# Experts' stage of a one-layer backbone kernel: the low half of U is made ahead of the gathered steps, the stage's first loads are asked for in another order, and its pools wait for their own bytes

## The chip, the cores and the metric

One NeuronCore of one Trainium2 chip runs the whole kernel. The metric is device time in microseconds (us) of one execution, the median of a few. The engines are TensorE (PE; its weight loads are shown as PEld), VectorE (DVE), ScalarE (ACT), GpSimd (POOL) and SyncE (SP). Each runs its own instructions in program order and waits on semaphores for the others. DMA transfers are asked for by SyncE and, for the gathers, by GpSimd; 16 DMA engines carry them.

## What is computed

One layer over 1024 tokens of width 1024: a mixer (state-space heads and a convolution group), and behind it a retrieval network over 16384 experts, each of which is one row of `u_tab` and one of `v_tab`. The change concerns the last part alone:

```python
q = (hf @ wq).reshape(t, PEER_HEADS, 2, PEER_KEY_DIM // 2)
s = einsum("thpd,hpkd->thpk", q, sub_keys)
sv, si = top_k(s, 16)                        # per half key, then over the 256 pairs
best, flat = top_k(cand, 16)                 # 8 heads x 16 experts for each token
gates = softmax(best)
act = gelu(einsum("pd,ped->pe", xb, u_tab[eb]), approximate=False)
out = einsum("pe,ped->pd", gb * act, v_tab[eb])
```

then `x + mod * out` and a final RMS norm.

## The kernel before, in words

The tokens lie in eight tiles of 128. In front of the experts' stage the **selection** finds each token's 128 experts and gates (`select`, L1016), for seven tiles; its pools `tp2`, `spl`, `gst` and two PSUM pools are closed before the stage opens its own. `prepare` (L994) already splits the activations (`hh2`, `hl2`) and multiplies expert block 0; it asks for U of blocks 0 to 3.

The **experts' stage** (L1241 on) has two kinds of work for two sets of tokens.

*Dense, for the first five tiles (640 tokens).* All 16384 experts are multiplied, in 128 blocks of 128, with gates that are zero where an expert was not chosen. A block's `In` step (L1358) has these parts: `load` brings U of the block (512 KB, SyncE), `split` makes its high half `uh` (ScalarE), `lower` its low half `ul` = u - uh (VectorE, L982), `gate` brings the gates of two blocks `gm` (640 KB, SyncE), `mm` multiplies (TensorE, 48 matmuls of 320 columns in groups of 8; the first 8 need `uh`, the next 8 `ul`), `post` is the gelu (ScalarE, L1392), `weigh` multiplies by the gates (VectorE, L1396) and makes the high half `wh` (ScalarE), `low` the low half `wl` (VectorE, L1402). An `Out` step (L1404) brings 256 KB of V, splits it into `vh` (ScalarE) and `vl` (VectorE, L61) and multiplies 15 times with 512 columns. `seq` (L1475) sets their order: 8 `In`, then for each of 16 groups 8 `Out`, one `In`, 8 `Out`, seven `In`.

*Gathered, for the last three tiles.* `gathered` (L1272) is a generator. For each token tile it asks GpSimd to gather 128 rows of `u_tab` (one expert of each token, 512 KB a request, L1281), lets VectorE multiply each with the activations h2 (L1303), and then does the same with rows of `v_tab` (L1315): 768 gathers, 5 buffers `gr`. The selection of the eighth tile (`choosing`, L1340) also runs here, in small pieces on VectorE and GpSimd; it reads its scores `s` from DRAM.

The order of every engine's queue is the order in which Python emits the instructions. `mm` of an `In` calls `advance(2, 18)`, that of an `Out` `advance(1, 11)` (L1347): as many pieces of the selection, and gathered steps in proportion to 18 and 11 (788 steps in 5066 units: 2.8 and 1.7 steps). Thus the gathered steps stand on VectorE's queue between `weigh` and `low` of the block before. The main loop (L1504) is:

```python
before.weigh()            # the In in front, if there is one
passed[type(x)] += 1
begin(In, "gate", 2)
x.mm()                    # TensorE, and advance() on VectorE and GpSimd
before.low()
begin(In, "lower", 1)     # ul of the next In
begin(In, "load", NU + 1)
x.post()
```

`begin(kind, what, far)` does that part for the steps up to `far` ahead. Blocks 0 to 3 are multiplied or prepared ahead of the loop, so the first `In` that multiplies in the loop is block 3, and block 4 is the first whose U is loaded in it.

A tile is given its place by its pool: the buffers lie in the order in which the names are first asked for. The stage's pools lie where the selection's lay, from the same byte on: `ep2` over `tp2` and part of `spl`, the gathers' `gp` over `gst`. In `tp2` the order is `iotx`, `v`, `ix`, `scr` (4 KB so far), `o1` (4 KB), `cand` (3.1 KB), `best`, `pos`, `posf`, `ef`, and so on. `gm` has two buffers of 5 KB for each partition, `v` three of 2 KB. By default the first use of a pool's memory waits until all users of the pools under it are through.

Of the kernel before, what the change touches and what calls it, by code (L numbers as in the profile page):

```python
# [8 lines left out]
F32 = mybir.dt.float32  # L9
# [6 lines left out]
PSUM = bass.MemoryType.PSUM  # L16
DRAM = bass.MemoryType.DRAM

P = 128
# [20 lines left out]
TH = TD // 2  # L40
NS = 7
NGB = 5
IN_US, OUT_US = 18, 11
NU, NV = 3, 3
GE = 8
# [27 lines left out]
def layer_kernel(ctx, tc, A, dbg=None):  # L73
# [293 lines left out]
    with ExitStack() as st:  # L367
# [126 lines left out]
        for n, c in enumerate(order):  # L494
# [13 lines left out]
            elif c >= 16 and c < 20:  # L508
                i = c - 16
# [458 lines left out]
    U = {}  # L968
# [6 lines left out]
    def split_u(u):  # L975
        uh = e2.tile([P, KD, P], F32R, name="uh")
        ul = e2.tile([P, KD, P], F32R, name="ul")
        nc.scalar.activation(uh, u, AF.Copy)  # L978
        return uh, ul, u

    def lower_u(uh, ul, u):
        nc.vector.tensor_tensor(ul, u, uh.bitcast(F32), op=OP.subtract)  # L982
        return uh, ul
# [255 lines left out]


    with ExitStack() as st:  # L1241
        ep2 = st.enter_context(tc.tile_pool(name="ep2", bufs=2))
        tp1 = st.enter_context(tc.tile_pool(name="tp1", bufs=1))
        wpl = st.enter_context(tc.tile_pool(name="wpl", bufs=GE + 1))
        gp = st.enter_context(tc.tile_pool(name="gp", bufs=NGB))
        psV = st.enter_context(tc.tile_pool(name="psV", bufs=1, space=PSUM))
        acc = h2T[:, :ND]
        h2, ac, spare = (h2T[:, ND + i] for i in range(3))
        spare_w, spare = spare, spare.rearrange("p (k t) -> p k t", t=P)
# [22 lines left out]
        def gathered():  # L1272
# [4 lines left out]
            def ask():  # L1277
                if asks:
                    t, b, e = asks.pop(0)
                    g = gp.tile([P, D], F32, name="gr")  # L1280
                    nc.gpsimd.indirect_dma_start(out=g, out_offset=None, in_=A[t],  # L1281
                                                 in_offset=bass.IndirectOffsetOnAxis(ap=idx[:, b, e:e + 1], axis=0))
                    rows.append(g)

            nc.sync.dma_start(h2, h2n_dram[:P, :])
            for _ in range(NGB - 2):
                ask()
            for b in range(NT - ND):
                act = ep2.tile([P, P], F32, name="act")
                wv = ep2.tile([P, P], F32, name="wv")  # L1290
# [29 lines left out]
            yield from done  # L1320

        steps = gathered()
        units = [0, 0]

        SE = {}

        def bring(z, hh):
            SE[z, hh] = tp1.tile([P, 4, P], F32, name="s", bufs=2)
            nc.sync.dma_start(SE[z, hh].rearrange("p a b -> p (a b)"), sc_dram[z - NS, hh])
# [8 lines left out]
            return tp1.tile([P, 2, TOPK], F32, name="ef"), heads(gates[:, z - ND], h0, 2)  # L1338

        def choosing():  # L1340
            bring(NS, 0)
            for z in range(NS, NT):
                yield from select(z, tp1, 2, scored, put)

        choice = choosing()

        def advance(n, us):  # L1347
# [128 lines left out]
        for g in range(NG):  # L1476
# [3 lines left out]
            seq += [Out(g, 1, i) for i in range(GE)]  # L1480
            if g + 1 < NG:
                seq += [In((g + 1) * GE + i) for i in range(1, GE)]
        early = [psV.tile([P, 512], F32, name=f"pv{i}")[:, :TH] for i in range(4)]
        for e in (1, 2):
            if e > 1:
                U[e] = lower_u(*split_u(U[e]))
            done[e] = multiply_u(*U.pop(e), early[2 * e - 2:2 * e])
        U[3] = lower_u(*split_u(U[3]))
        passed = {In: 0, Out: 0}
        queues = {(kind, what): iter([x for x in seq if isinstance(x, kind)]) for kind, what in  # L1490
                  ((In, "load"), (In, "split"), (In, "lower"), (In, "gate"), (Out, "load"), (Out, "split"))}
# [2 lines left out]
        def begin(kind, what, far):  # L1494

            while begun[kind, what] < passed[kind] + far:
                begun[kind, what] += 1
                x = next(queues[kind, what], None)
                if x:
                    getattr(x, what)()  # L1500

        begin(In, "load", NU + 1)
        begin(Out, "load", NV)
        for n, x in enumerate(seq):  # L1504
            begin(In, "split", 2)
            begin(Out, "split", 2)
            begin(Out, "load", NV + 2)
            before = seq[n - 1] if n and isinstance(seq[n - 1], In) else None
            if before:
                before.weigh()  # L1510
            passed[type(x)] += 1
            begin(In, "gate", 2)
            x.mm()
            if before:
                before.low()
            begin(In, "lower", 1)
            begin(In, "load", NU + 1)
            x.post()
        for _ in steps:
            pass  # L1520
# [75 lines left out]
```

## Time and profile before

| | before |
|---|---|
| median of 3 runs | 3130.14 us (3124.53 to 3130.31) |
| profiled execution | 3129.54 us, span 3127.7 us |
| TensorE busy | 2841.5 us, 91% |
| VectorE busy | 2632.5 us, 84% |
| GpSimd, ScalarE busy | 1713.4 us, 1011.7 us |
| DMA | 722.65 MB, 231 GB/s over the span |

By stretches of the experts' stage:

| us from the span's start | TensorE busy | VectorE busy | granted clock | DMA share |
|---|---|---|---|---|
| 1203 to 1260 | 38.37 of 57 | 33.33 | 0.78 | 0.72 |
| 1260 to 1700 | 404.26 of 440 | 376.30 | 0.96 | 0.84 |
| 1700 to 3040 | 1322.57 of 1340 | 1155.31 | 1.00 | 0.94 |
| 3040 to 3128 | 60.26 of 88 | 57.38 | 0.83 | 0.37 |

All times are from one profiled execution and count from its start. A busy TensorE is not TensorE at its peak: matmuls overlap, and their ends are modelled. "Waited for" names the instruction whose semaphore came last. The granted clock is the share of TensorE's full rate: 1.0 is 2.4 GHz, 0.5 is 1.2 GHz.

### The profile page before, as it was taken

How to read it: one execution, taken by the hardware profiler on the slowest of the kernel's cores; microseconds unless marked ns; L12 is line 12 of the kernel's file. 1: busy time of each engine (PE TensorE's matmuls, PEld its weight loads, DVE VectorE, ACT ScalarE, POOL GpSimd, SP SyncE). 2: the span in 40 equal slices, each digit the busy share in tenths (PEclk: the TensorE clock that was granted, in tenths of full speed). 3: DMA queues.
4: the chain of work that ended last, by engine and by line, in shares of the span. 5: the costliest groups of instructions: out<-in, count | busy, mean ns of one | idle time of the engine just before them, and what ended most of it. 6: DMA issues, size and time to landing. Idle time of an engine off the chain costs nothing.

```text
span 3127.7 us, 41600 instructions
## 1 busy us (share of the span) xinstructions
PE 2841.5 (91%) x14905; PEld 2381.7 (76%) x14905; DVE 2632.5 (84%) x4956; ACT 1011.7 (32%) x1584; POOL 1713.4 (55%) x1361
## 2 busy tenths in 40 slices
PE   7999777998888875999989999999999999999996
PEld 3777676764555555887878988998998898898885
DVE  5898788559999997889888888888888888888886
ACT  3224323333555652232222222222222322222222
POOL 0221454425676774666666666565566555556663
PEclk8999999999999887999999999999999999999998
DMA  6111355250222125888879999999998998999983
GB/s 209 61 40 42 112 150 184 81 188 7 115 108 108 55 122 199 286 277 314 297 273 326 320 336 339 328 334 326 327 334 315 328 349 314 334 335 322 327 290 127
DMA packets 334543, 722.65 MB, mean 231 GB/s; under 512 B 24560, under 2 KB 167168, under 8 KB 333056
## 3 DMA queue, kind: packets, MB, share of 16 engines
q0 software_dynamic: 112176, 408.47, 36.8%
q1 hardware_dynamic: 222160, 311.53, 29.0%
q8 instruction: 117, 1.92, 0.2%
q14 instruction: 90, 0.74, 0.1%
HBM read 658.56 MB, written 61.35 MB: 230 GB/s over the span
## 4 chain that ended last, share of the span: by engine, by line
PE 44%; DVE 29%; issue 10%; DMA 8%; POOL 6%; ACT 2%; SPq 0%; DVEq 0%; POOLq 0%; ACTq 0%
PE pa L990 18%; PE pv L1428 5%; PE pv L1429 5%; PE pv L1427 5%; POOL gr L1281 4%; DMA gr<-in_peer_u_dram,idx 4%; DVE cfm L408 3%; DVE o L1211 3%; PE pa L68 3%; DVE ob L1203 2%; PE pq L947 2%; DVE oh L1081 2%; DMA gr<-in_peer_v_dram,idx 2%; DVE gr L1303 1%; DVE h2T L1315 1%
## 5 line engine op out<-in xcount | busy, mean ns | idle before, releaser
L1281 POOL DMA_INDIRECT gr<-in_peer_v_dram,idx x384 | 537.6, 1400 | 325.5 <-DVE h2T L1315 219.1
L1281 POOL DMA_INDIRECT gr<-in_peer_u_dram,idx x384 | 523.8, 1364 | 347.9 <-DVE gr L1303 262.5
L1428 PE MATMUL pv<-vl,wh 128*128 128x512 f32 x1280 | 513.4, 401 | 26.0 <-DVE vl L61 25.9
L1315 DVE SCALAR_TENSOR_TENSOR h2T<-gr,wv,h2T 128x1024 f32<-128x1024 f32 x381 | 495.7, 1301 | 38.3 <-DMA gr<-in_peer_v_dram,idx 31.5
L1427 PE MATMUL pv<-vh,wl 128*128 128x512 f32 x1280 | 510.6, 399 | 7.2 <-ACT vh L60 7.0
L1303 DVE SCALAR_TENSOR_TENSOR gr<-gr,h2T 128x1024 f32<-128x1024 f32 x384 | 463.9, 1235 | 57.5 <-DMA gr<-in_peer_u_dram,idx 52.8
L1429 PE MATMUL pv<-vh,wh 128*128 128x512 f32 x1280 | 510.7, 399 | 0.0
L60 ACT ACTIVATE vh<-v 128x512 fp32r<-128x512 f32 x256 | 161.8, 632 | 682.6 <-PE pv L1429 656.1
L990 PE MATMUL pa<-hh,ul 128*128 128x320 f32 x2000 | 340.3, 313 | 40.1 <-DVE ul L982 39.2
L990 PE MATMUL pa<-hl,uh 128*128 128x320 f32 x2000 | 336.8, 311 | 8.3 <-ACT uh L978 8.3
L990 PEld LDWEIGHTS pa<-hh,ul 128*128 128x128 f32 x2000 | 306.6, 190 | 45.4 <-DVE ul L982 44.4
L990 PE MATMUL pa<-hh,uh 128*128 128x320 f32 x2000 | 337.6, 311 | 0.0
L990 PEld LDWEIGHTS pa<-hl,uh 128*128 128x128 f32 x2000 | 307.8, 190 | 11.3 <-ACT uh L978 8.6
L1428 PEld LDWEIGHTS pv<-vl,wh 128*128 128x128 f32 x1280 | 243.2, 190 | 92.4 <-DVE vl L61 35.7
L990 PEld LDWEIGHTS pa<-hh,uh 128*128 128x128 f32 x2000 | 307.5, 190 | 0.0
L1392 ACT ACTIVATE ga<-pa 128x320 f32<-128x320 f32 x252 | 110.0, 438 | 594.7 <-PE pa L990 571.0
L1427 PEld LDWEIGHTS pv<-vh,wl 128*128 128x128 f32 x1280 | 243.6, 190 | 66.4 <-ACT vh L60 8.2
L1429 PEld LDWEIGHTS pv<-vh,wh 128*128 128x128 f32 x1280 | 243.4, 190 | 57.8
L1205 POOL TENSOR_TENSOR o<-ob,tr 128x512 f32<-128x512 bf16 x160 | 216.5, 1355 | 110.7 <-DVE ob L1203 99.4
L1189 PEld LDWEIGHTS pg<-o,o 128*128 128x128 f32 x1280 | 173.9, 207 | 132.5 <-issue 66.4
L61 DVE TENSOR_TENSOR vl<-v,vh 128x512 fp32r<-128x512 f32 x256 | 184.4, 721 | 105.1 <-ACT vh L60 104.1
L1189 PE MATMUL pg<-o,o 128*128 128x128 f32 x1280 | 187.4, 297 | 78.8 <-DVE o L1211 53.9
(357 smaller groups left out, 4510.3 us busy)
## 6 DMA issues: line engine op xcount, KB each, us to landing
v<-in_peer_v_dram SPq DMA_DIRECT2D x256, 256.0 KB
u<-in_peer_ut_dram SPq DMA_DIRECT2D x87, 512.0 KB
g_dram<-stg SPq DMA_DIRECT2D x10, 4096.0 KB
gm<-g_dram SPq DMA_DIRECT2D x64, 640.0 KB
h2T<-in_peer_ut_dram SPq DMA_DIRECT2D x41, 512.0 KB
ld<-in_ada_w_dram SPq DMA_DIRECT2D x24, 512.0 KB
w<-in_w_in_t_dram SPq DMA_DIRECT2D x21, 512.0 KB
raw<-in_ada_w_dram SPq DMA_DIRECT2D x8, 1024.0 KB
```

Of the source, the lines that this page charges most:

```text
L60: nc.scalar.activation(hi, src, AF.Copy)
L61: (eng or nc.vector).tensor_tensor(lo, src, hi.bitcast(F32), op=OP.subtract)
L990: nc.tensor.matmul(pa[half], x[:, k], y[:, k, half * TH:half * TH + TH], start=t == 0 and k == 0, stop=t == 2 and k == KD - 1)
L1189: nc.tensor.matmul(pg[:, j], o2[:, j], o1[:, j], start=True, stop=True)
L1205: nc.gpsimd.tensor_tensor(o2.rearrange("p t j -> p j t"), ob, tr[:, 1, None, ts].to_broadcast([P, P, 4]), op=OP.mult)
L1281: nc.gpsimd.indirect_dma_start(out=g, out_offset=None, in_=A[t], in_offset=bass.IndirectOffsetOnAxis(ap=idx[:, b, e:e + 1], axis=0))
L1303: nc.vector.scalar_tensor_tensor(g, g, 1.0, h2, op0=OP.mult, op1=OP.mult, accum_out=act[:, e:e + 1])
L1315: nc.vector.scalar_tensor_tensor(ac, g, wv[:, e:e + 1], ac, op0=OP.mult, op1=OP.add)
L1392: nc.scalar.activation(self.ga[:, half * TH:half * TH + TH], self.pa[half], AF.Gelu)
L1427: nc.tensor.matmul(Out.pv[t], wl[:, sl], self.vh, start=i == 0, stop=False)
L1428: nc.tensor.matmul(Out.pv[t], wh[:, sl], self.vl, start=False, stop=False)
L1429: nc.tensor.matmul(Out.pv[t], wh[:, sl], self.vh, start=False, stop=i == GE - 1)
```

## The change

Four things move; nothing is added to or taken from the arithmetic.

- The five pools of the stage are opened with `reuse_waits="tile"`: the first use of a buffer waits for the users of the bytes under it, not for all users of the pools that lay there.
- `gathered` now stops once behind its first requests (h2 on SyncE, three gathers on GpSimd), and it is run to that point where it is made; the first scores of the eighth tile (`bring(NS, 0)`) are asked for there too.
- The first gates (blocks 0 to 2, two `gm` tiles) are asked for ahead of the first V tiles, and all these loads ahead of the multiplications of blocks 1 and 2 in the program.
- In the loop, `lower` and the load of U stand between `weigh` of the block before and `mm`.

```diff
@@ -1239,11 +1239,11 @@
 
 
     with ExitStack() as st:
-        ep2 = st.enter_context(tc.tile_pool(name="ep2", bufs=2))
-        tp1 = st.enter_context(tc.tile_pool(name="tp1", bufs=1))
-        wpl = st.enter_context(tc.tile_pool(name="wpl", bufs=GE + 1))
-        gp = st.enter_context(tc.tile_pool(name="gp", bufs=NGB))
-        psV = st.enter_context(tc.tile_pool(name="psV", bufs=1, space=PSUM))
+        ep2 = st.enter_context(tc.tile_pool(name="ep2", bufs=2, reuse_waits="tile"))
+        tp1 = st.enter_context(tc.tile_pool(name="tp1", bufs=1, reuse_waits="tile"))
+        wpl = st.enter_context(tc.tile_pool(name="wpl", bufs=GE + 1, reuse_waits="tile"))
+        gp = st.enter_context(tc.tile_pool(name="gp", bufs=NGB, reuse_waits="tile"))
+        psV = st.enter_context(tc.tile_pool(name="psV", bufs=1, space=PSUM, reuse_waits="tile"))
         acc = h2T[:, :ND]
         h2, ac, spare = (h2T[:, ND + i] for i in range(3))
         spare_w, spare = spare, spare.rearrange("p (k t) -> p k t", t=P)
@@ -1285,6 +1285,7 @@
             nc.sync.dma_start(h2, h2n_dram[:P, :])
             for _ in range(NGB - 2):
                 ask()
+            yield
             for b in range(NT - ND):
                 act = ep2.tile([P, P], F32, name="act")
                 wv = ep2.tile([P, P], F32, name="wv")
@@ -1320,6 +1321,7 @@
             yield from done
 
         steps = gathered()
+        next(steps)
         units = [0, 0]
 
         SE = {}
@@ -1338,10 +1340,10 @@
             return tp1.tile([P, 2, TOPK], F32, name="ef"), heads(gates[:, z - ND], h0, 2)
 
         def choosing():
-            bring(NS, 0)
             for z in range(NS, NT):
                 yield from select(z, tp1, 2, scored, put)
 
+        bring(NS, 0)
         choice = choosing()
 
         def advance(n, us):
@@ -1480,27 +1482,28 @@
             seq += [Out(g, 1, i) for i in range(GE)]
             if g + 1 < NG:
                 seq += [In((g + 1) * GE + i) for i in range(1, GE)]
+        passed = {In: 0, Out: 0}
+        queues = {(kind, what): iter([x for x in seq if isinstance(x, kind)]) for kind, what in
+                  ((In, "load"), (In, "split"), (In, "lower"), (In, "gate"), (Out, "load"), (Out, "split"))}
+        begun = dict.fromkeys(queues, 0)
+
+        def begin(kind, what, far):
+
+            while begun[kind, what] < passed[kind] + far:
+                begun[kind, what] += 1
+                x = next(queues[kind, what], None)
+                if x:
+                    getattr(x, what)()
+
+        begin(In, "gate", 3)
+        begin(In, "load", NU + 1)
+        begin(Out, "load", NV)
         early = [psV.tile([P, 512], F32, name=f"pv{i}")[:, :TH] for i in range(4)]
         for e in (1, 2):
             if e > 1:
                 U[e] = lower_u(*split_u(U[e]))
             done[e] = multiply_u(*U.pop(e), early[2 * e - 2:2 * e])
         U[3] = lower_u(*split_u(U[3]))
-        passed = {In: 0, Out: 0}
-        queues = {(kind, what): iter([x for x in seq if isinstance(x, kind)]) for kind, what in
-                  ((In, "load"), (In, "split"), (In, "lower"), (In, "gate"), (Out, "load"), (Out, "split"))}
-        begun = dict.fromkeys(queues, 0)
-
-        def begin(kind, what, far):
-
-            while begun[kind, what] < passed[kind] + far:
-                begun[kind, what] += 1
-                x = next(queues[kind, what], None)
-                if x:
-                    getattr(x, what)()
-
-        begin(In, "load", NU + 1)
-        begin(Out, "load", NV)
         for n, x in enumerate(seq):
             begin(In, "split", 2)
             begin(Out, "split", 2)
@@ -1510,11 +1513,11 @@
                 before.weigh()
             passed[type(x)] += 1
             begin(In, "gate", 2)
+            begin(In, "lower", 1)
+            begin(In, "load", NU + 1)
             x.mm()
             if before:
                 before.low()
-            begin(In, "lower", 1)
-            begin(In, "load", NU + 1)
             x.post()
         for _ in steps:
             pass
```

## Rows read from the trace of the kernel before

**Rows 1.** The page, part 1: busy us (share of the span) and instructions.
```profile
PE 2841.5 (91%) x14905; PEld 2381.7 (76%) x14905; DVE 2632.5 (84%) x4956; ACT 1011.7 (32%) x1584; POOL 1713.4 (55%) x1361
```

**Rows 2.** TensorE's waits, 1205 to 1262: waiter, for whom: us, times, longest.
```profile
PE pa L990 <- DVE ul L982: 10.1, 1, 10.1
PE pa L990 <- ACT uh L978: 8.3, 1, 8.3
```

**Rows 3.** The same view, 1262 to 1700.
```profile
PE pa L990 <- DVE ul L982: 20.4, 5, 7.3
PE pv L1428 <- DVE vl L61: 13.4, 5, 5.5
```

**Rows 4.** The same view, 1700 to 3040.
```profile
PE pa L990 <- DVE ul L982: 8.8, 11, 1.7
```

**Rows 5.** SyncE in order of time: start us, us, instruction. Start of the stage.
```profile
1202.83 0.33 SPq L972 DMA_DIRECT2D u<-in_peer_ut_dram  x1
1211.33 9.19 SPq L1413 DMA_DIRECT2D v<-in_peer_v_dram  x5
1220.58 1.69 SPq L1371 DMA_DIRECT2D gm<-g_dram  x2
...
1233.52 0.62 SPq L1285 DMA_DIRECT2D h2T<-h2n_dram  x1
```

**Rows 6.** VectorE in order of time, same stretch; in brackets its wait before.
```profile
1210.94 0.22 DVE L1099 CAST idx<-ef 128x128 int32<-128x128 f32 x1
...
1228.25 0.82 DVE L1396 TENSOR_TENSOR ga<-ga,gm 128x640 f32<-128x640 f32 x1 [8.09 <-DMA gm<-g_dram]
...
1245.14 1.22 DVE L982 TENSOR_TENSOR ul<-u,uh 128x1024 fp32r<-128x1024 f32 x1
```

**Rows 7.** TensorE in order of time, same stretch.
```profile
1233.86 2.50 PE L990 MATMUL pa<-hl,uh 128*128 128x320 f32 x8 [8.35 <-ACT uh L978]
1246.41 2.50 PE L990 MATMUL pa<-hh,ul 128*128 128x320 f32 x8 [10.05 <-DVE ul L982]
```

**Rows 8.** GpSimd in order of time, same stretch.
```profile
1207.80 1.61 POOL L1083 TENSOR_TENSOR oh<-oh,cand 128x160 f32<-128x160 f32 x2 [0.32 <-DVE oh L1081]
```

**Rows 9.** Stretches: length, engines' busy us, granted clock, DMA share, GB/s.
```profile
1194.00:1203.00 9.00, 4.24 (x15) 3.56 (x14) 8.90 (x28) 0.00 (x0) 6.01 (x6) 0.51 0.02 5
...
1228.00:1234.00 6.00, 0.14 (x1) 0.14 (x1) 3.94 (x5) 3.89 (x8) 0.00 (x0) 0.52 0.56 200
```

**Rows 10.** DMA queues, 1216 to 1222: packets, MB, share (q0 GpSimd's, q1 SyncE's).
```profile
q0 software_dynamic: 437, 1.61, 70.5%
q1 hardware_dynamic: 347, 0.64, 29.6%
```

**Rows 11.** ScalarE in order of time, start of the stage.
```profile
1218.81 0.63 ACT L60 ACTIVATE vh<-v 128x512 fp32r<-128x512 f32 x1 [2.85 <-DMA v<-in_peer_v_dram]
...
1220.75 0.77 ACT L1392 ACTIVATE ga<-pa 128x320 f32<-128x320 f32 x2
...
1232.75 1.06 ACT L978 ACTIVATE uh<-u 128x1024 fp32r<-128x1024 f32 x1
```

**Rows 12.** TensorE's waits, 1480 to 1520.
```profile
PE pa L990 <- DVE ul L982: 7.6, 3, 4.7
```

**Rows 13.** VectorE in order of time, around 1505.
```profile
1501.06 0.81 DVE L1396 TENSOR_TENSOR ga<-ga,gm 128x640 f32<-128x640 f32 x1
...
1510.03 1.23 DVE L1303 SCALAR_TENSOR_TENSOR gr<-gr,h2T 128x1024 f32<-128x1024 f32 x1 [1.77 <-DMA gr<-in_peer_u_dram,idx]
...
1511.91 1.22 DVE L982 TENSOR_TENSOR ul<-u,uh 128x1024 fp32r<-128x1024 f32 x1
```

**Rows 14.** The chain that ended last: start us, us, instructions. TensorE, two pieces.
```profile
1349.58 7.05 PE pa L990 x48
...
1391.47 7.94 PE pa L990 x40
```

**Rows 15.** VectorE's waits, 1700 to 3040.
```profile
DVE ga L1396 <- ACT ga L1392: 48.8, 60, 2.1
```

More of the change, by code (lines that the diff above doesn't have):

```diff
@@ L1482, in layer_kernel @@
                 seq += [In((g + 1) * GE + i) for i in range(1, GE)]
[L1483 to L1488, printed above, removed]
         passed = {In: 0, Out: 0}
@@ L1500, in begin @@
                     getattr(x, what)()
+        begin(In, "gate", 3)
         begin(In, "load", NU + 1)
         begin(Out, "load", NV)
+        early = [psV.tile([P, 512], F32, name=f"pv{i}")[:, :TH] for i in range(4)]
+        for e in (1, 2):
+            if e > 1:
+                U[e] = lower_u(*split_u(U[e]))
+            done[e] = multiply_u(*U.pop(e), early[2 * e - 2:2 * e])
+        U[3] = lower_u(*split_u(U[3]))
         for n, x in enumerate(seq):
```

## The prediction

> **What bounds the kernel now.** I read the page first: TensorE is busy for 91% of the span [rows 1], and in the experts' stage (the last 1900 us) the other engines feed it. So the second view is what TensorE waited for, cut into three stretches. At the start of the stage it waits twice, 8.3 us for `uh` and 10.1 us for `ul` [rows 2]; from 1262 to 1700 it waits 20.4 us for `ul` in 5 pieces and 13.4 us for `vl` [rows 3]; from there to 3040 only 8.8 us for `ul` in 11 pieces [rows 4]. The stage's price above pure matmul time lies in these waits, and the sum is made of them. The third view is the order of time on each queue at the start. The reader should see there that nothing computes slowly: everything stands in line behind something that was asked for late. SyncE asks for `v` at 1211.33, for `gm` at 1220.58, for h2 at 1233.52 [rows 5]; VectorE's first gate multiplication starts at 1228.25 after 8.09 us of waiting for `gm`, and `ul` of expert block 4 at 1245.14, behind three gathered steps that waited for h2 [rows 6]; TensorE resumes with `uh` at 1233.86 and with `ul` at 1246.41 [rows 7].
>
> **Edit 1, loads in another order, own bytes only (the start).** Moved on SyncE: h2 and the first `s` block come to the front, then both `gm` tiles, then the three `v`. On GpSimd three gathers are asked for earlier in the program, but its queue holds nothing between their old and new place, so they start where they do now, behind the last `oh` product (1207.80 + 1.61 = 1209.4) [rows 8].
> When can SyncE start? Its load of block 3 stands ahead of all this and goes out at 1202.83 [rows 5]; h2, `s` and `gm` 0 can follow from 1203.2. Own bytes: by the tile sizes and the order of first request, `gm` 0 lies over selection tiles that are read for the last time before 1203; the data it reads has been written, for the DMA engines are at 0.02 from 1194 to 1203 [rows 9]. So these three, 1.4 MB, land by about 1210 in time that is idle now. `gm` 1 reaches into `cand`, which the last `oh` product reads: it waits to 1209.4, and everything behind it on SyncE with it. `v` 0 lies over tiles read to about 1209.5, `v` 1 over `ef`, read by the cast at 1210.94 [rows 6]. Hence **v gains almost nothing from the own bytes**: it goes out at about 1210 to 1211.5 against 1211.33, with 0.66 MB of `gm` 1 now ahead of it, while five gathers (2.6 MB) move as well.
> How the two queues share the engines is shown between 1216 and 1222: gathers 1.61 MB, SyncE's queue 0.64 MB [rows 10]. At that ratio SyncE gets some 110 GB/s until the gathers are through, so `gm` 1 and two `v` (1.18 MB from 1211) land at about 1222; now the second `vh` starts at 1218.81. Then that `vh`, ScalarE's table load and the gelu (1218.81 to 1221.52 now, 2.7 us [rows 11]) and the first gate multiplication at about 1224.7 instead of 1228.25: no wait for `gm` is left, but 3.5 us later `v` is the new last wait. From there the present spacing holds: `uh` of block 4 is made 4.5 us after the first multiplication (1232.75 against 1228.25) [rows 6, 11], so from about 1229.2 to 1230.3; block 4's load follows `v` 4 and lands at about 1228.
> The Trainium skill (DMA: Bandwidth & Descriptors, Queues, rings and completion order) says that each DMA engine takes the queues in turn, packet by packet. Read as equal halves this would bring `v` some 4 us sooner and the sum to 3082; the row does not agree, its split is 70 to 30.
>
> **Edit 2, `ul` ahead of the gathered steps.** In the iteration of block n VectorE now does: gate multiplication of n-1, the 2 to 3 gathered steps and the selection's pieces, `wl`, then `ul` of n+1. After the change `ul` stands second. Nothing is added; about 1.2 us change places. At the start `ul` of block 4 then ends at 1231.5, without h2 or `s` in its way. TensorE needs it 8 matmuls after `uh`, so it goes on from 1230.3. Its first matmuls run at the low clock (granted 0.52 from 1228 to 1234 [rows 9], the 1.2 GHz level) in both kernels, since it stands still before them in both. Now the slow piece that leads into steady work begins with the second eight, at 1246.4; then it begins with the first eight, at 1230.3. That is 16.1 us, less the eight that are already done now, which cost 1.2 us at full clock (8 matmuls, a sixth of the 7.05 us of 48 [rows 14]): **15 us at the start**. Bounds: 12 if `v` and block 4 come 3 us later still; 20 if TensorE does not stop at all (8.3 + 10.1 and, as below, 2.1 for the slow matmuls).
>
> From 1262 to 1700 the example is a run of three stalls between 1480 and 1520, 7.6 us, the last of 4.7 [rows 12]. Before that last one VectorE made the gate multiplication at 1501.06, then stood in the gathered steps (the last started at 1510.03 after waiting for its row), and only then made `ul`, at 1511.91 [rows 13]. Put behind the multiplication, `ul` is ready by about 1503 and TensorE does not stop. But the gathers come no sooner. VectorE reaches the next multiplication at about 1512 and the next `ul` ends at about 1514; TensorE started on that `ul` at about 1513.2; without the stalls it would have done so 7.6 us sooner, and would want the next one 7.05 us [rows 14] after that, at about 1512.6. So of 7.6 us about 1.4 come back one block later: four fifths stay. **20.4 us x 0.8 = 16 us**; bounds 6 (the lag is handed on) and 20.4.
>
> After a long stall the next matmuls are slow too. The 40 matmuls behind the stall at 1391 took 7.94 us, where 48 undisturbed ones take 7.05, which is 5.87 for 40 [rows 14]: 2.07 us. For three such stalls (this one, the one just worked through and the longest, of 7.3 us [rows 3]) 6.2 us, of which I take **5**; bounds 1 and 6.2.
>
> From 1700 on the 8.8 us [rows 4] are pieces of at most 1.7 us, and `ul` moves ahead by two to three steps of about 1.2 us: they vanish, less what is handed on: **8 us**, bounds 4 and 8.8.
>
> **What the moved `ul` may cost.** It now waits for `uh`, which no `ul` does in this trace. ScalarE makes `uh` right behind the gelu that also releases the multiplication; `uh` takes 1.06 us [rows 11], the multiplication 0.82 [rows 6]. So VectorE can stop for some 0.25 us in each block, and queued behind it are the gathered steps, which give GpSimd its buffers back. That is hidden by the idle time that VectorE has at the multiplication: 48.8 us over some 95 blocks from 1700 to 3040, 0.5 a block [rows 15]. Where it lags, `uh` is done long before. Taken at nothing; 0.25 x 124 = 31 us if that cover were gone. `wl` comes up to 1.2 us later; its reader is an output block that comes after the rest of its group, so nothing. The load of `u` for block n+4 is issued behind the earlier `ul` and so comes up to 5 us sooner; it is three blocks early already and takes no more bytes. The first `gm` requests are moved, not added. On SyncE the load of `u` passes only what the steps ask for between, the selection's `s` blocks and two output rows' stores, which nothing waits for at once.
>
> **The sum.** 15 + 16 + 5 + 8 = 44 us. The profiled execution took 3129.5 us (span 3127.7 and 1.8 around it), the median of the runs is 3130.1, so they may be used alike: 3130 - 44 = **3086 us**.
>
> **Rivals.**
> (a) More: the start runs without a stop, all `ul` waits vanish: 20 + 20.4 + 6.2 + 8.8 = 55, 3075 us. For it: the `ul` waits are explained by order alone. Against it: `v` stays tied to 1210 and later.
> (b) The lag is handed on. The gathers are as late as before, and what TensorE no longer waits for at `ul` it waits for at `vl` in the output blocks, where 13.4 us are waited already [rows 3]. The start keeps 15, the rest 4: 3111 us. Against it: each gate multiplication ties VectorE to TensorE, and in a group of 48 matmuls (7.05 us) VectorE has about 6.3 us of work: 0.82 for the multiplication, 1.22 for `ul` [rows 6], as much as the multiplication for `wl`, and by the code's pacing 2.8 steps of 1.23 [rows 13].
> (c) The start gains nothing: the small pieces of `gm` 1 ahead of `v` hold it back by some 15 us, or the own bytes free nothing. Only edit 2 is left: 29 us, 3101 us. Against it: h2, `s` and `gm` 0 land in idle DMA time.
> (d) Slower. The new wait of `ul` for `uh` is paid in all 124 blocks, 31 us, and brings the steps behind it late, so that the stalls stay; only the start's 15 is gained: 3130 + 31 - 15 = 3146 us. This decides from the point where VectorE's idle time per block falls under 0.25 us; it is 0.5 in the steady part.
>
> **How the numbers follow.** Forecast (3078 to 3095) 0.60; (a) 0.13; (b) 0.14; (c) 0.09; (d) 0.04. The range takes in (a) and (b): 3067 to 3112. A measurement of this kernel tells about 0.2% from no change, that is 6 us; all cases but (d) are more than that on the fast side. I leave 0.05 for mishaps in which the parts cancel: faster 0.91, same 0.05, slower 0.04.
>
> **What would show it.** In the changed kernel's trace: SyncE asks for h2 and `gm` between 1203 and 1210 and for `v` at 1210 to 1212; the first gate multiplication waits for `v` and the gelu, not for `gm`, and starts near 1225; TensorE's wait for `uh` near 1225 falls from 8.3 to about 5, and the following one for `ul` is gone. From 1262 to 1700 the waits of TensorE for `ul` sum to some 4 us instead of 20.4, with those for `vl` not above 18. After 1700 they are near nothing, and VectorE shows many short waits of `ul` for `uh`, about 0.25 us. I am wrong if the waits for `vl` grow by what those for `ul` lose (b), if `v` lands past 1230 (c), or if those short waits go along with later gathered steps and TensorE stalls in every group (d).

## The result, and the profile after

| | before | after |
|---|---|---|
| median of 5 runs | 3130.14 us (3124.53 to 3139.56) | 3106.25 us (3098.53 to 3110.93) |
| ratio, with 95% interval | 1 | 0.9916 [0.9892, 0.994] |
| profiled execution, span | 3129.54, 3127.7 us | 3110.93, 3109.2 us |
| first matmul of the stage (L990) | 1202.8 us | 1207.6 us |
| from there to the end | 1925.0 us | 1901.5 us |
| TensorE, VectorE busy | 2841.5, 2632.5 us | 2846.0, 2628.3 us |

The change makes the kernel faster, by 24 us of the 44 that were forecast. The profiled execution of after is the slowest of its five, 4.7 us over their median, so a few microseconds between two traces are scatter. In this trace the stage begins 4.8 us later than before, in work that the change doesn't touch. So the two traces are compared from the stage's first matmul on, and cut at the same matmuls, which follow one another in the same order in both: the **start** up to the fifth eight of block 4, the **middle** from there to the 14400th of 14905 matmuls, and the **end**.

| us | start | middle | of it, TensorE's waits | of it, slow matmuls | end |
|---|---|---|---|---|---|
| before | 49.8 | 1743.7 | 51.3 | 23.0 | 131.5 |
| after | 32.0 | 1738.3 | 43.1 | 25.7 | 131.2 |

"Slow matmuls" is the time by which matmuls were over 25% further apart than the median one of their kind, without the waits. The start gained 17.8 us, the middle 5.4, the end nothing.

**The start.** SyncE in order of time in the kernel after (start us, us, engine, line, transfer):

```profile
1207.67 0.33 SPq L972 DMA_DIRECT2D u<-in_peer_ut_dram  x1
1208.12 0.36 SPq L1285 DMA_DIRECT2D h2T<-h2n_dram  x1
1208.58 0.37 SPq L1331 DMA_DIRECT2D s<-sc_dram  x1
1209.38 5.28 SPq L1373 DMA_DIRECT2D gm<-g_dram  x2
1214.71 10.06 SPq L1415 DMA_DIRECT2D v<-in_peer_v_dram  x5
```

A row of several requests (x2, x5) also holds SyncE's waits between them. The two requests for `gm` take 0.37 us each, at 1209.38 and 1214.29; between them SyncE waited for GpSimd's last `oh` product (SyncE's waits: who, for whom, us, times, longest):

```profile
SPq L1373 <- POOL oh L1083: 4.5, 1, 4.5
```

Then VectorE, ScalarE and TensorE, each in order of time; in brackets the idle time before the instruction and what ended it:

```profile
1225.81 0.83 DVE L1398 TENSOR_TENSOR ga<-ga,gm 128x640 f32<-128x640 f32 x1 [1.39 <-ACT ga L1394]
...
1233.42 1.23 DVE L982 TENSOR_TENSOR ul<-u,uh 128x1024 fp32r<-128x1024 f32 x1 [2.05 <-ACT uh L978]
```

```profile
1223.06 0.63 ACT L60 ACTIVATE vh<-v 128x512 fp32r<-128x512 f32 x1 [1.98 <-DMA v<-in_peer_v_dram]
...
1232.33 1.06 ACT L978 ACTIVATE uh<-u 128x1024 fp32r<-128x1024 f32 x1 [1.90 <-DMA u<-in_peer_ut_dram]
```

```profile
1233.44 2.50 PE L990 MATMUL pa<-hl,uh 128*128 128x320 f32 x8 [3.06 <-ACT uh L978]
1235.73 1.69 PE L990 MATMUL pa<-hh,ul 128*128 128x320 f32 x8
```

The gates are asked for ahead of `v`, and VectorE's first gate multiplication waits 1.39 us for the gelu and no longer 8.09 for `gm` [rows 6]. It comes 18.2 us after the stage's first matmul, before 25.5. `ul` of block 4 follows `uh` at once, and TensorE stops once, for 3.06 us, where it stopped for 8.3 and for 10.1 [rows 2].

**The middle.** TensorE's waits over the same matmuls, first before (1252.6 to 2996.3), then after (1239.6 to 2977.9): engine, line, what it waited for, us in total, times, longest.

```profile
PE pa L990 <- DVE ul L982: 27.4, 15, 7.3
PE pv L1428 <- DVE vl L61: 21.1, 14, 5.5
PE pv L1427 <- ACT vh L60: 2.0, 1, 2.0
```

```profile
PE pv L1430 <- DVE vl L61: 29.0, 14, 5.4
PE pa L990 <- DVE ul L982: 7.3, 3, 5.1
PE pv L1429 <- ACT vh L60: 6.5, 4, 2.8
```

The waits for `ul` fell by 20.1 us, as the order explains; those for `vl` and `vh` grew by 12.4, and the sum fell by 8.2. VectorE's own waits, in the same stretches, before and then after:

```profile
DVE ga L1396 <- ACT ga L1392: 63.3, 68, 3.3
DVE gr L1303 <- DMA gr<-in_peer_u_dram,idx: 52.8, 50, 5.1
DVE h2T L1315 <- DMA gr<-in_peer_v_dram,idx: 28.6, 26, 6.5
```

```profile
DVE gr L1304 <- DMA gr<-in_peer_u_dram,idx: 70.2, 57, 5.8
DVE h2T L1316 <- DMA gr<-in_peer_v_dram,idx: 45.0, 34, 6.3
DVE ga L1398 <- ACT ga L1394: 20.6, 34, 1.8
```

VectorE now waits less for the gelu (63.3 to 20.6) and more for gathered rows (81.4 to 115.2). A TensorE that does not stop for `ul` delivers the next gelu sooner; VectorE then reaches its gathered steps sooner, and the rows are not there. That reading is argued from the rows, but it holds in every trace below that has edit 2 and otherwise the same stage: there VectorE waits 98 to 115 us for rows and 21 to 30 for the gelu, without edit 2 81 to 83 and 63 to 66.

Late rows and TensorE's waits go together. In the kernel after, of the 36.3 us that TensorE waited for `ul` or `vl` in the middle, 33.1 (13 of 17 waits) have a wait of VectorE of over 1 us for a row in the 15 us ahead of that `ul` or `vl`; such stretches make up 31% of the middle. The longest wait for `vl` shows how; VectorE, then TensorE:

```profile
1567.79 1.28 DVE L1316 SCALAR_TENSOR_TENSOR h2T<-gr,wv,h2T 128x1024 f32<-128x1024 f32 x1 [6.33 <-DMA gr<-in_peer_v_dram,idx]
...
1569.73 0.69 DVE L61 TENSOR_TENSOR vl<-v,vh 128x512 fp32r<-128x512 f32 x1
```

```profile
1570.47 0.80 PE L1430 MATMUL pv<-vl,wh 128*128 128x512 f32 x1 [5.45 <-DVE vl L61]
```

**The place of the prediction's example.** In front of the matmuls that stalled for 4.7 us near 1513 [rows 12, 13] TensorE no longer waits (they start at 1494.50), but one input block later, 48 matmuls further on, it stands for 5.1 us. VectorE, then TensorE, then GpSimd ahead of it, in order of time in the kernel after:

```profile
1498.04 1.23 DVE L1304 SCALAR_TENSOR_TENSOR gr<-gr,h2T 128x1024 f32<-128x1024 f32 x1 [1.45 <-DMA gr<-in_peer_u_dram,idx]
...
1502.90 1.23 DVE L1304 SCALAR_TENSOR_TENSOR gr<-gr,h2T 128x1024 f32<-128x1024 f32 x1 [3.63 <-DMA gr<-in_peer_u_dram,idx]
...
1504.79 0.82 DVE L1398 TENSOR_TENSOR ga<-ga,gm 128x640 f32<-128x640 f32 x1
1505.53 1.22 DVE L982 TENSOR_TENSOR ul<-u,uh 128x1024 fp32r<-128x1024 f32 x1
```

```profile
1506.80 2.50 PE L990 MATMUL pa<-hh,ul 128*128 128x320 f32 x8 [5.10 <-DVE ul L982]
1509.10 2.33 PE L990 MATMUL pa<-hh,uh 128*128 128x320 f32 x8
```

```profile
1479.50 1.68 POOL L1281 DMA_INDIRECT gr<-in_peer_u_dram,idx  x1 [1.08 <-DVE gr L1304]
1485.23 2.65 POOL L1083 TENSOR_TENSOR oh<-oh,cand 128x160 f32<-128x160 f32 x2 [4.04 <-DVE oh L1081]
1488.03 1.78 POOL L1281 DMA_INDIRECT gr<-in_peer_u_dram,idx  x1 [0.16 <-issue]
```

`ul` stands right behind the multiplication, as meant, but the multiplication itself is late: two gathered steps of the block before waited 1.45 and 3.63 us for their rows. One reason stands in GpSimd's queue: between 1479.5 and 1488.0 it asked for no gather, since it waited 4.04 us for VectorE's `oh` and then made two products of the selection. In the order of the requests the two late rows were asked for at 1490.12 and 1491.97, behind that gap; the second then took 10.9 us to land. So of the 7.6 us that the prediction worked through, 5.1 came back one block later.

### The profile page after: what moved, and what is told of

It reads as the page before. It is cut to its first block, busy times and chain, and to the rows that moved or that the text cites. A ratio compares the mean times of both kernels' runs of the same rounds, so it can differ in the third digit from the quotient of the medians.

```text
span 3109.2 us, 41552 instructions
## 1 busy us (share of the span) xinstructions
PE 2846.0 (92%) x14905; PEld 2385.5 (77%) x14905; DVE 2628.3 (85%) x4956; ACT 1011.2 (33%) x1584; POOL 1705.3 (55%) x1361
## 3 DMA queue, kind: packets, MB, share of 16 engines
q0 software_dynamic: 112176, 408.47, 36.9%
## 5 line engine op out<-in xcount | busy, mean ns | idle before, releaser
L1281 POOL DMA_INDIRECT gr<-in_peer_u_dram,idx x384 | 516.5, 1345 | 340.6 <-DVE gr L1304 253.3
L990 PE MATMUL pa<-hh,ul 128*128 128x320 f32 x2000 | 335.6, 310 | 7.3 <-DVE ul L982 7.3
L990 PE MATMUL pa<-hl,uh 128*128 128x320 f32 x2000 | 336.0, 310 | 3.3 <-ACT uh L978 3.1
L990 PE MATMUL pa<-hh,uh 128*128 128x320 f32 x2000 | 334.9, 310 | 0.0
L990 PEld LDWEIGHTS pa<-hl,uh 128*128 128x128 f32 x2000 | 306.6, 189 | 6.5 <-ACT uh L978 3.3
L990 PEld LDWEIGHTS pa<-hh,ul 128*128 128x128 f32 x2000 | 304.9, 189 | 8.1 <-DVE ul L982 8.1
L990 PEld LDWEIGHTS pa<-hh,uh 128*128 128x128 f32 x2000 | 304.5, 188 | 0.0
```

The lines of the kernel that those rows point to most:

```text
L990: nc.tensor.matmul(pa[half], x[:, k], y[:, k, half * TH:half * TH + TH], start=t == 0 and k == 0, stop=t == 2 and k == KD - 1)
```

## The experiments

The profiled executions of the kernels below were cut at the same matmuls as above. Medians are from other chips than the first result, so kernels are compared by their ratio to the kernel before on the same chip; the kernel after itself was timed on the first chip alone.

**Edit 1 alone, and edit 2 alone.** The first is the kernel after with `lower` and the load of U back in their old place:

```diff
             begin(In, "gate", 2)
-            begin(In, "lower", 1)
-            begin(In, "load", NU + 1)
             x.mm()
             if before:
                 before.low()
+            begin(In, "lower", 1)
+            begin(In, "load", NU + 1)
             x.post()
```

> Edit 1 alone: requests reordered, pools wait for their own bytes, but the low half of U stays behind the gathered steps. Theory H (the two edits do different things: edit 1 shortens the start, edit 2 frees the low half of U, and most of what edit 2 frees is handed on to other waits): at the start the low half of block 4 still stands behind three gathered steps, so TensorE gains some 6 us there, and from 1260 to 1700 its waits for the low half of U sum to about 20 us as before: 3124 us. Rival S (the start is edit 1's work and edit 2 adds little): 3112 us, with 15 us gained at the start.

The second is the kernel before with the reverse of this diff and nothing else.

> Edit 2 alone, on the kernel before: low half of U and the load of U ahead of the multiplication, old order of requests, pools as before. Theory H: the first gate multiplication still waits for its gates until about 1228, but the low half of block 4 no longer waits for h2: TensorE's 10 us wait at the start goes, and later the same waits remain as with both edits: 3130 - 11 - 8 = 3111 us. Rival S: only the part behind the start is gained, 3122 us.

| | ratio | start | middle | TensorE's waits in it | slow matmuls |
|---|---|---|---|---|---|
| before | 1 | 49.8 | 1743.7 | 51.3 | 23.0 |
| edit 1 alone | 0.997 [0.995, 0.9991] | 35.5 | 1744.9 | 54.9 | 20.7 |
| edit 2 alone | 0.9943 [0.9922, 0.9963] | 36.4 | 1746.1 | 51.4 | 25.1 |
| both | 0.9916 [0.9892, 0.994] | 32.0 | 1738.3 | 43.1 | 25.7 |

TensorE's waits in the middle with edit 2 alone:

```profile
PE pv L1428 <- DVE vl L61: 36.8, 20, 6.2
PE pa L990 <- DVE ul L982: 11.0, 4, 4.2
PE pv L1427 <- ACT vh L60: 3.4, 3, 1.9
```

`ul` lost 16.4 us (27.4 to 11.0), `vl` gained 15.7, and the sum is what it was, 51.4 against 51.3: in this trace the lag was handed on whole. In all four traces that have edit 2 and `vl` in its old place (this one, after, and the next two runs) `ul` is at 3.6 to 11.0 and `vl` at 29.0 to 36.8, in the two without edit 2 `ul` at 27.4 and 31.2 and `vl` at 21.1 and 21.3. All of TensorE's waits together are 43.1 to 51.4 us with edit 2, and 51.3 and 54.9 without it. So the shift from `ul` to `vl` is shown, and only some 7 us went, on the average. At the start each edit alone gains most of what both do (14.3 and 13.4 of 17.8): the first brings `gm` and h2, the second lets `ul` pass the steps that wait for h2, so the second to be made finds little left. For edit 1 alone the theory had put 6 us there and its rival 15; the rival was right on the start, the theory on the waits for `ul`, which stay. The middle's 5.4 us with both edits is no more than one profiled execution differs from another (the five runs of after lie within 12.4 us), and neither edit alone shows any of it in its trace. The ratios, which rest on all runs, give edit 1 alone 9 us (3 to 16) and edit 2 alone 18 (12 to 24); the latter leaves room for some 4 us behind the start, and not for 29.

**Without the own bytes.** The kernel after, with the pools opened as before:

```diff
-        ep2 = st.enter_context(tc.tile_pool(name="ep2", bufs=2, reuse_waits="tile"))
+        ep2 = st.enter_context(tc.tile_pool(name="ep2", bufs=2))
```

and so for the other four pools.

> Both edits, but the five pools wait for all users of the pools under them. Theory H: V could not go out before 1210 anyway, since SyncE stands in line behind the second gates tile; the scores and gates come some 5 us later, and the start loses 2 to 4 us: 3109 us. Rival: the own bytes carry the gain of the start: 3118 us or more.

Ratio 0.9937 [0.9917, 0.9957]. The start takes 38.3 us instead of 32.0: TensorE stands still for 7.8 us, for the gelu, which stands on ScalarE's queue behind `vh` and its wait for `v`; `vh` starts 24.0 us behind the stage's first matmul (1203.2), and with the own bytes the second `vh` starts after 15.5. `v` is late because SyncE's request for `s`, which stands ahead of `gm` and `v`, waited 7.5 us for VectorE's last piece of the selection (`idx`, L1099). ScalarE in order of time in this kernel:

```profile
1227.23 1.17 ACT L60 ACTIVATE vh<-v 128x512 fp32r<-128x512 f32 x2 [14.98 <-DMA v<-in_peer_v_dram]
```

So the own bytes are worth some 6 us of the start in this order of requests, where 2 to 4 were expected. The total can't be told from that of after: the intervals overlap, and the middle of this trace is 4.6 us shorter (1733.7).

**With the load of U back.** The kernel after, but the load stays behind `mm`:

```diff
             begin(In, "lower", 1)
-            begin(In, "load", NU + 1)
             x.mm()
             if before:
                 before.low()
+            begin(In, "load", NU + 1)
```

> Both edits, but the load of U stands behind the multiplication again; the low half stays ahead. Theory H: the load is three blocks early and nobody waits for it: within 3 us of the changed kernel, 3106 us. Rival D: the earlier loads of U crowd the gathers, whose waits on VectorE grew from 53 to 74 us after 1700; with the load back these waits fall to some 55 us and the time to about 3098 us.

Ratio 0.9912 [0.988, 0.9944], start 31.9, waits in the middle 46.7: the same as after within the scatter. VectorE's waits for rows after 1700 fall from 73 to 64 us, where the rival had 55, but TensorE's waits and the time don't fall with them: the earlier loads of U show neither a gain nor a loss.

**Fewer pieces on GpSimd.** Eleven small additions of the selection (L1035, four times in the stage) stand between GpSimd's gather requests. They go to VectorE:

```diff
-            stair(nc.gpsimd, ixf, cand[:, 1], UPPER + LOWER)
+            stair(nc.gpsimd if nh == NH else nc.vector, ixf, cand[:, 1], UPPER + LOWER)
```

> The changed kernel with one more move: in the eighth tile's selection the 11 small additions that GpSimd makes in one burst (7.1 us at their longest, four bursts) go to VectorE. Theory G (VectorE's lag is the lateness of the gathered rows, and between 1260 and 1700 they are late because GpSimd asks for them behind that burst): VectorE's waits of 4 to 6 us for a row at the four bursts go; TensorE's waits in that stretch fall from 29.5 to about 13 us, and the stage's time by 12 to 18 us. Rival V (VectorE itself has too much work): 4 us more work on VectorE, so TensorE's waits rise and the time is 2 to 5 us above the changed kernel.

The line's instructions in the kernel after and then here (ns least, median, most):

```profile
L1035 POOL TENSOR_TENSOR cand<-ix x44: 195/262/1267, 1268.2 to 1561.5; 128x8 f32<-128x8 f32 x16, 128x16 f32<-128x16 f32 x12, 128x6 f32<-128x6 f32 x8, 128x4 f32<-128x4 f32 x8
```

```profile
L1035 DVE TENSOR_TENSOR cand<-ix x44: 152/158/228, 1264.4 to 1542.0; 128x8 f32<-128x8 f32 x16, 128x16 f32<-128x16 f32 x12, 128x6 f32<-128x6 f32 x8, 128x4 f32<-128x4 f32 x8
```

Ratio 0.9863 [0.9836, 0.989]: 0.5% below after, though VectorE, the busier engine, has 44 instructions more. Its waits for rows in the middle fall from 115.2 to 85.6 us. The time is as Theory G had it, the way there is not: TensorE's waits hardly fall (43.1 to 41.4, and from 1260 to 1700 only from 29.5 to 26.0 where 13 was expected); the slow matmuls do, from 25.7 to 17.7 us. The longest wait for `vl` is 3.2 instead of 5.4, that for `ul` 5.6 instead of 5.1. Why the slow matmuls fall is not shown. The Trainium skill (GPSIMD Engine Reference, Engine selection) puts an elementwise operation with two inputs at about twice VectorE's time on GpSimd; here the median is 1.7 times (262 to 158 ns), but the longest is 1267 ns.

**Half of VectorE's gathered work.** Both gathered steps work on 512 of 1024 columns; the gathers stay whole:

```diff
-scalar_tensor_tensor(g, g, 1.0, h2, ...)
+scalar_tensor_tensor(g[:, :512], g[:, :512], 1.0, h2[:, :512], ...)
-scalar_tensor_tensor(ac, g, wv[:, e:e + 1], ac, ...)
+scalar_tensor_tensor(ac[:, :512], g[:, :512], wv[:, e:e + 1], ac[:, :512], ...)
```

> The changed kernel, but each gathered step on VectorE takes the first 512 columns of its row alone, so the last three tiles' results leave out half of every dot product and half of every sum. The gathers are whole. VectorE's work falls by some 470 us. Theory G (gathers late, not VectorE overloaded): VectorE still stands at rows that have not landed; TensorE's waits for vl and ul behind the start fall by less than half, from 43 to 25 us or so. Rival V: they nearly vanish, under 10 us, and the time falls by 35 us or more.

Ratio 0.9745 [0.9721, 0.9769]. The time falls as Rival V had it (by 1.7% of the kernel against after), though VectorE's work falls by 393 us and not 470. TensorE's waits in the middle fall to 15.5 us, between the two theories, while VectorE still waits 128.6 us for rows. All 13.9 us that TensorE still waits for `ul` or `vl` come behind a wait of VectorE of over 1 us for a row, in the 15 us ahead. So the rows are late either way, and less of that reaches TensorE where VectorE has more slack to make it good.

**Cover for `vl`.** If the lag only moves to the next half that is not covered, that half must be covered as well. In an output block the five products with `vl` go behind the ten with `vh`:

```diff
                 for t in range(ND):
                     sl = slice(t * P, t * P + P)
                     nc.tensor.matmul(Out.pv[t], wl[:, sl], self.vh, start=i == 0, stop=False)
-                    nc.tensor.matmul(Out.pv[t], wh[:, sl], self.vl, start=False, stop=False)
-                    nc.tensor.matmul(Out.pv[t], wh[:, sl], self.vh, start=False, stop=i == GE - 1)
+                    nc.tensor.matmul(Out.pv[t], wh[:, sl], self.vh, start=False, stop=False)
+                for t in range(ND):
+                    sl = slice(t * P, t * P + P)
+                    nc.tensor.matmul(Out.pv[t], wh[:, sl], self.vl, start=False, stop=i == GE - 1)
```

> The changed kernel, but the five products with vl in an output block come behind the ten with vh, so that vl is wanted 2.3 us later. No work is added. Theory H (what is freed at ul is handed on to the next wait without cover, vl): with 2.3 us of cover the waits for vl of up to that length go: after 1700 they fall from 13.6 to about 4 us, between 1260 and 1700 from 29.5 to about 18; 3106 - 18 = 3088 us. Rival C (the waits are conserved: what is not waited at vl is waited one step later): they sum to 43 us as before, under another name, and the time stays at 3106 us.

Then the same with the eleven additions on VectorE, as above:

> Both of the last moves on the changed kernel: vl wanted 2.3 us later, and the 11 small additions on VectorE. By G and H together TensorE's waits between 1260 and 1700 fall to about 6 us and after it to 4: 3106 - 30 = 3076 us. By C or V nothing is gained beyond the better of the two alone.

| | ratio | TensorE's waits, middle | slow matmuls |
|---|---|---|---|
| after | 0.9916 [0.9892, 0.994] | 43.1 | 25.7 |
| `vl` last | 0.9855 [0.9836, 0.9875] | 35.9 | 17.6 |
| `vl` last, additions on VectorE | 0.9823 [0.9801, 0.9846] | 25.9 | 11.2 |

Both times are close to what the theories gave, but the waits fall by less: to 35.9 where some 22 was expected, and to 25.9 where 10 was. The rest of the gain is in the slow matmuls.

TensorE's waits in the middle of the last one, then VectorE's for rows:

```profile
PE pv L1433 <- DVE vl L61: 12.8, 8, 2.5
PE pa L990 <- DVE ul L982: 6.6, 4, 3.1
PE pv L1429 <- ACT vh L60: 6.5, 4, 3.4
```

```profile
DVE gr L1304 <- DMA gr<-in_peer_u_dram,idx: 68.8, 58, 3.7
DVE h2T L1316 <- DMA gr<-in_peer_v_dram,idx: 43.7, 51, 4.0
```

VectorE waits for rows as long as in the kernel after (112.5 us), but less of it reaches TensorE. This is the best version of the study: 3080.64 us (median of 4) beside 3136.24 for the kernel before, 1.8% less.

**The same two moves without the change.** The kernel before, with `vl` last and the additions on VectorE, neither edit 1 nor edit 2.

> The kernel before (neither edit) with the two later moves: vl wanted 2.3 us later, the 11 small additions on VectorE. Theory H (low half of U ahead pays once vl has cover too): the start loses its 18 us again and the waits for ul behind the start stay at 20 to 30 us, since nothing covers them: 3080 + 18 + 15 = 3113 us. Rival N (edit 2 is worth nothing behind the start, with or without cover for vl): 3080 + 18 = 3098 us, and the waits for ul behind the start are under 15 us.

Ratio 1.0019 [1.0005, 1.0033]: 0.2% slower than before, where on top of the change they gave 0.9%. Neither theory had that (3113 and 3098 us). TensorE's waits in the middle:

```profile
PE pa L990 <- DVE ul L982: 44.3, 21, 10.3
PE pv L1431 <- DVE vl L61: 6.9, 9, 1.5
```

The waits for `vl` fall from 21.1 to 6.9, and those for `ul` grow from 27.4 to 44.3. It looks like the mirror image of edit 2 alone, but it is not the same lag under another name: up to 1700 `ul` is waited for as long as before (20.5 and 20.4), and all of the growth lies after. TensorE's waits from 1700 to the end of the middle, before and then here:

```profile
PE pa L990 <- DVE ul L982: 7.0, 10, 1.3
```

```profile
PE pa L990 <- DVE ul L982: 23.7, 16, 2.1
```

Of the 23.7 us, 18.2 come within 15 us behind the five sums of a finished output group (L1448; 3.9 of the 7.0 before). With the products with `vl` last, a group's five sums are all finished only at its end; VectorE waits for that, makes the five sums, and the gathered steps and `ul` stand behind them:

```profile
1709.21 3.08 DVE L1448 TENSOR_TENSOR h2T<-h2T,pv 128x512 f32<-128x512 f32 x5 [1.57 <-PE pv L1431]
1719.16 1.22 DVE L982 TENSOR_TENSOR ul<-u,uh 128x1024 fp32r<-128x1024 f32 x1
```

```profile
1720.43 2.31 PE L990 MATMUL pa<-hh,ul 128*128 128x320 f32 x8 [2.11 <-DVE ul L982]
```

VectorE waits 32.7 us in the middle for the last product in this way, and not at all in the kernel before. In the best version it does so too (28.5 us), but there `ul` stands ahead of the gathered steps, and no wait for `ul` is left after 1700. From this kernel the best one differs by the change alone, and in ratios by 2.0% (1.0019 to 0.9823), some 61 us of 3130, where the change by itself gave 0.8%: the change is worth far more where `vl` comes last. That this is edit 2's doing and not edit 1's rests on these rows; the two were not parted on this kernel.

**Is there more in the pacing, or in `ul`?** On the best version: units of 20 and 10 for the gathered steps instead of 18 and 11; `ul`'s eights third instead of second in each group of 24 matmuls; and both.

```diff
-IN_US, OUT_US = 18, 11
+IN_US, OUT_US = 20, 10
```

> The fastest so far (both edits, vl last, additions on VectorE), with the gathered steps paced 20 to 10 for input and output blocks instead of 18 to 11: 3.1 and 1.6 steps instead of 2.8 and 1.7. Theory H: output blocks have the shorter cover, so moving steps out of them takes from the waits for vl (12.7 us) about a third: 3076 us. Rival: input blocks are then full (6.8 of 7.05 us of VectorE work) and the waits for ul rise by more: 3085 us.

```diff
-            for t, (x, y) in enumerate(((uh, hl2), (ul, hh2), (uh, hh2))):
+            for t, (x, y) in enumerate(((uh, hl2), (uh, hh2), (ul, hh2))):
```

> The fastest so far, and in an input block the eight products with ul come third instead of second in each half, so that ul is wanted 1.2 us later. Theory H: of the 6.6 us that are waited for ul between 1260 and 1700 some 3 go: 3077 us. Rival C (conserved): the same 3 us appear at vh or vl: 3080 us.

> Both of these on the fastest so far: by Theory H 3073 us, with ul's longer cover carrying the fuller input blocks; by the rivals 3080 to 3085 us.

Ratios 0.9886 [0.986, 0.9912], 0.9831 [0.9812, 0.9849] and 0.9884 [0.9864, 0.9903], where the best version had 0.9823. More gathered steps beside the `In` blocks cost 0.6%, more than either theory had: the waits in the middle rise from 25.9 to 36.9, most of the growth for `vh` (6.5 to 13.5) and `ul` (6.6 to 9.4). More cover for `ul`, beyond what edit 2 gives, changes nothing (26.4), and does not carry the fuller input blocks either. Neither of these two moves takes away what is left.

## Why the prediction was right or wrong, step by step

- **SyncE's order, `v` not sooner: right.** h2, `s` and `gm` went out first and `v` last, 7.1 us behind the stage's first matmul (1214.71 - 1207.6), before 8.5 [rows 5]. The second `vh` came 15.5 us behind it, before 16.0 [rows 11]. The wait of the second `gm` for the last `oh` product, and `v` behind it, came as forecast. I had feared that `gm` ahead of `v` would cost `v` 3 us; it cost nothing. "v gains almost nothing from the own bytes" is right against the kernel before, but in the new order `v` would go out 4 us later without them (11.2 us behind the first matmul).
- **The start, 15 us: right, 17.8 measured.** The single stop for `uh` is 3.06 us; I had put it at about 5. What ended it was not the chain of multiplications that the sum followed: `uh` waited 1.90 us for block 4's load of U, which the prediction had landing at about 1228 (it came at 1227.5, counted from the first matmul as before) and just not last. Without the own bytes 6 us of it are lost, with edit 1 alone 3.5, with edit 2 alone 4.4.
- **The new wait of `ul` for `uh`, taken at nothing: right.** No wait of `ul` for `uh` stands among VectorE's waits from 1262 to 2978, not even the many short ones of 0.25 us that I had named as a sign. Rival (d) is excluded.
- **The earlier load of U, taken at nothing: not contradicted** by the run that puts it back.
- **"Four fifths stay" (16 us), the slow matmuls (5) and the waits after 1700 (8): wrong.** Of these 29 us the middle shows 5.4, and edit 2 alone shows none in its trace. This is the step that failed, and what happened is near rival (b), to which I gave 0.14: its 3111 us lie 5 from the measured 3106, the forecast's 3086 lie 20. That 3106 lies in the range of 3067 to 3112 owes nothing to the forecast's mechanism; the range was drawn wide enough to take in (b). The waits for `ul` did go: 20.4 to 7.3 from 1262 to 1700, and to none from there to 2978. But I followed the lag only as far as the next `ul` (1.4 of 7.6 us "come back one block later", where 5.1 did), on one example, and let VectorE take up the rest as slack. Two things were missing there. First, the next reader in line after a group of `In` is an output block, whose `vl` stood second of three products, with one matmul of cover. Second, VectorE's time in those blocks is not only its work of 6.3 in 7.05 us: it stops for rows, and it stops longer when it comes sooner. My argument against (b), "each gate multiplication ties VectorE to TensorE", did not hold: with TensorE no longer late the tie kept VectorE back less, and its waits moved from the gelu (less 42.7 us) to the rows (more 33.8 us).
- **The slow matmuls** did not fall (23.0 to 25.7 us, where 5 us were to go): waits over 2 us were 6 before and 9 after. Their number alone does not set the slow matmuls, though, for with the additions on VectorE there are 9 as well and 17.7 us.
- **The signs I had named** did their work: `vl` "not above 18" from 1262 to 1700 came to 18.0, with `vh` 3.9 on top, and "I am wrong if the waits for `vl` grow by what those for `ul` lose" is what the row of edit 2 alone says. Another was missed: the waits for `ul` from 1262 to 1700 were to sum to some 4 us, and sum to 7.3.

What stays open: why the rows are late, whether by late requests on GpSimd or by the transfers themselves (the DMA share after 1700 was 0.94 in the kernel before), which no run here parts; and whether the middle of after is really 5 us shorter than that of edit 2 alone, or whether that is scatter. More gather buffers, or a third pair of `vh` and `vl`, were not tried.

## What to carry to other kernels

When an engine in the middle (here VectorE) serves several readers in a fixed order and is itself late, bringing one product forward moves the wait to the next product without cover; sum the waits of all its products before and after, not only the one that is moved. Cover all of them (put the matmuls that need the late half behind those that don't) or remove the lag's source, and look what the cover itself makes late, as `vl` last did with the sums. Test the edits together: here the change alone gave 0.8%, the two later moves alone nothing, and all together 1.8%.

## What the runs showed of the hardware

The clock's part is plain at the stall shown above. Stretches of the kernel after: the wait, the first eight behind it, the next 17 matmuls, the 42 after those (busy us and instructions of each engine, then the granted clock, DMA share, GB/s):

```profile
1501.70:1506.80 5.10, 0.00 (x0) 0.00 (x1) 3.90 (x6) 1.14 (x2) 1.28 (x1) 0.94 0.85 320
1506.80:1509.10 2.30, 2.30 (x8) 2.30 (x9) 2.30 (x6) 2.27 (x3) 0.13 (x1) 0.50 0.78 273
1509.10:1513.20 4.10, 4.10 (x17) 4.10 (x17) 4.03 (x10) 2.90 (x6) 2.72 (x2) 0.53 0.63 207
1513.20:1519.00 5.80, 5.80 (x42) 5.80 (x41) 5.80 (x9) 2.13 (x3) 2.53 (x2) 1.00 0.97 326
```

The granted clock is 0.50, the 1.2 GHz level, behind the wait of 5.1 us and not in it. 24 matmuls take 6.4 us (1506.80 to 1513.21) where 24 later ones take 3.5 (1513.21 to 1516.72): this wait costs 5.1 + 2.9 us. A longer wait costs more, but hardly more for each microsecond: over the middles of all 14 traces, waits of 1 to 2 us (144.0 us in all) are followed by 50.5 us of slow matmuls, waits of over 4 us (157.5 us) by 62.4. This is an estimate, with slow matmuls within 12 us behind a wait put down to it. So several short waits are not clearly cheaper than one long one of the same sum.

Unexpected too was how long one request can stand on SyncE. At the start of the kernel after most loads of U and that of h2 took 0.33 to 0.42 us each; in the kernel before one load of U took ten times that, and the requests behind it came later by as much:

```profile
1222.31 4.37 SPq L972 DMA_DIRECT2D u<-in_peer_ut_dram  x1
```

What held it is not shown.
